# Second mixer's last output product by token halves, embedding matmuls back in the scan, the next stage begins with products of the left tokens

## The chip, the core and the metric

The kernel runs on one core of a Trainium2 chip. The metric is the device time of one execution in microseconds (us); of several runs the median counts.

## What is computed

One inference step of a two-layer decoder trunk for 512 prompt tokens and 64 sample tokens (8 sequences of 8) that share the weights; model width 1024, all in f32. Layer 0 has a mixer of two parallel heads (HGRN2 and RG-LRU), layer 1 a Mamba-2 mixer. Cut to what matters here:

```python
for i in range(DEPTH):                                   # 2 layers
    xn = _rmsnorm(x, W['g_mix'][i])
    mix = _even_mixer(xn, ...) if i % 2 == 0 else _odd_mixer(xn, ...)
    x = x + mix
    x = x + _swiglu(_rmsnorm(x, W['g_ffn'][i]), w1, w3, w2)
    x = x + _ple(x, p[i], W['ple_up'][i], W['ple_gate'][i], W['g_ple'][i])
y = _rmsnorm(x, W['g_final'])

# the end of _odd_mixer: a norm by each of 4 groups, then the out product
yg = y.reshape(B, L, G_C, D_INNER_C // G_C)
yg = yg * lax.rsqrt(jnp.mean(yg * yg, axis=-1, keepdims=True) + EPS)
out = (yg.reshape(B, L, D_INNER_C) * W['ssm_gnorm'][j]) @ W['ssm_out'][j]

def _swiglu(x, w1, w3, w2): return (jax.nn.silu(x @ w1) * (x @ w3)) @ w2
def _ple(x, p_i, w_up, w_gate, g):
    return _rmsnorm(jax.nn.sigmoid(x @ w_gate) * (p_i @ w_up), g)
```

## The kernel before

Activations lie features by tokens: `x[0]` to `x[7]` are 128 features by 576 tokens, and each product goes by two halves of 288 tokens (`half(s)`; the left half is s = 0). A product in f32 is made of three matmuls of fast type: every operand is split into a high and a low part, and high by high, low by high and high by low are added in PSUM. `wsplit` (L170) splits a weight tile of 128 x 1024, high part `whi` on ScalarE (L173), low part `wlo` on VectorE or GpSimd (L174); `split_to` does so with activations.

The order of the instructions is set by a scheduler of the language, engine by engine; code order, tile pools and their buffer counts are its input. An engine takes its own instructions strictly in that order.

`odd_mixer` (L705) runs 16 units of the scan (four groups of four). In a unit ScalarE makes `E`, the exponentials of the decay, VectorE multiplies it (L956), TensorE makes `yp` from it (L967), VectorE and GpSimd make `xs` from that, and ScalarE and VectorE split it into `xah` and `xal`, the operands `ya` of the out product. After a group's last unit its squares are summed (`acc`, `ssq` on TensorE), `ry` is a power on GpSimd (L236), and `rbc` on TensorE (L242) broadcasts it to all partitions; ScalarE copies it to SBUF (`rb`). `group_out` makes the out product of a group: for each of eight 128-feature blocks m 24 matmuls (both halves), the evacuation `t<-mm,rb` on VectorE (L348) and the add to `x` on GpSimd (L349). The table `OUT_AT` says behind which unit the group's product is written; the last group's stands behind unit 15, the last.

`ple_up` (L1227) makes the embedding product `p_i @ w_up`, 96 matmuls in each layer with evacuations `ev<-mm` on ScalarE (L1244). Its result is wanted only after the FFN. In layer 1 it is written behind the whole mixer and its operands are called `xb`.

`ffn` (L1042) makes the SwiGLU with a Strassen-like scheme: seven products replace eight, made of sums and differences of quarters of the activations (`b11`, `b21` from the left tokens, `b2`, `b1`, `b3`, `b4`, `b22` from differences or right tokens) and of the weights. The scaled quarters (x times the norm's weights, L1074, on VectorE) are `hh`; their splits are `bh` and `bl`. The norm factor `r` of the token is multiplied in afterwards, so that a product can run ahead of it. One product is 24 matmuls; the products' PSUM tiles are `mmx`, `mmy` and `mmz`, and `u` is a sum of weight quarters. Before, the first FFN products that TensorE takes stand behind the broadcast `rbc` of the norm factor.

Of the kernel before, what the change touches and what calls it, by code (L numbers as in the profile page):

```python
# [12 lines left out]
F = mybir.dt.float32  # L13
# [30 lines left out]
AHEAD, LAST, STEPS, UP_CUT = 4, 6, (3, 2), 6  # L44
PLE_V = [(0, 1, 2, 3, 4, 6), (0,)]
OUT_AT = {4: [(0, range(8))], 8: [(1, range(8))],
          12: [(2, range(0, 4))], 13: [(2, range(4, 6))], 14: [(2, range(6, 8))], 15: [(3, range(8))]}
XRB = 1
GT = [[4 * g, 4 * g + 1, 4 * g + 2, 4 * g + 3, 16 + g, 20 + g] for g in range(NG)]
LEVELS = (64, 32, 16, 8, 4, 2, 1)  # L50
# [29 lines left out]
def trunk(ctx, tc, a, stop=None):  # L80
# [21 lines left out]
    def pcol(name, i=0, n=1):  # L102
        return par[:, PAR[name] + i:PAR[name] + i + n]
# [29 lines left out]
    def bank(name="s", tag="s"):  # L133
        return pq.tile([P, 512], F, tag=tag, name=name)

    def singles(pool, tag):
        while True:
            yield [pool.tile([P, HF], R, tag=tag + t_, name=tag + t_, bufs=KD) for t_ in "hl"]
# [82 lines left out]
    def chunk(c):  # L221
        return slice(c * P, (c + 1) * P) if c < NCH else slice(SEQ, T)

    def rnorm(accs, n, lo, hi, outs):
        w = hi - lo
        nch = -(-w // P)
        last = w - (nch - 1) * P
        ps = bank("ssq")
        for i, acc in enumerate(accs):
            for c in range(nch):  # L230
                o = min(c * P, w - P)
                sums = PE.matmul(ps[:, c:c + 1], acc[:, o:o + P], ones[:, :1], start=(i == 0 and c == 0),  # L232
                                 stop=(i == len(accs) - 1 and c == nch - 1))
        ms, y = (tp.tile([P, nch], F, tag=n_, name=n_) for n_ in ("ms", "ry"))
        V.tensor_scalar(ms, ps[:, :nch], 1.0 / n, EPS, op0=OP.mult, op1=OP.add)
        G.tensor_tensor(y, ms, c_("mhalf", 1).to_broadcast([P, nch]), op=OP.pow)  # L236
        for b0 in range(0, w, 512):
            b1 = min(w, b0 + 512)
            pb = bank("rbc")
            for c0 in range(b0, b1, P):  # L240
                c1 = min(w, c0 + P)
                bc = PE.matmul(pb[:, c0 - b0:c1 - b0], y[:, c0 // P:c0 // P + 1].to_broadcast([P, P]), ident[:, P - (c1 - c0):],  # L242
                          start=True, stop=True)
            for out, sc in outs:
                S.activation(out[:, lo + b0:lo + b1], pb[:, :b1 - b0], AF.Copy, scale=sc)
        return sums.ins, bc.ins, pb

    def half(s):
        return slice(s * HF, (s + 1) * HF)
# [84 lines left out]
    def square_add(acc, src, first, eng=V):  # L334
        if first:
            S.activation(acc, src, AF.Square)
        else:
            sq = tmp("t2", 2)[:, :src.shape[-1]]
            one = S.activation(sq, src, AF.Square)
            two = eng.tensor_tensor(acc, acc, sq, op=OP.add)  # L340
            return one.ins, two.ins
# [33 lines left out]
    def even_mixer():  # L375
        xin = XIn("g_mix", 0)
        w_in, w_out = a["w_ein"], a["w_eout"]
        with ExitStack() as es:
# [323 lines left out]
                        next(fill[todo.pop(0)], None)  # L702
            run(mix_out(w_out, 0, split_out(oa, pairs(ac, "xc"))))

    def odd_mixer(xin, first):  # L705
        acts, r = xin.acts, xin.r
        w_in, w_out = a["w_sin"], a["w_sout"]
        with ExitStack() as es:
# [288 lines left out]
            def group_out(q, ms):  # L997
                run(mix_out(w_out, 4 * q.g, q.ya, q.rg, ms, q.marks if q.g == NG - 1 else ()))

            groups, xs, zs = {}, {}, {}  # L1000
            last_ya = singles(ac, "xa")
            units = 4 * NG

            def feed(u):
# [12 lines left out]
            for u in range(1 + GLOOK):  # L1017
                gate(u)
            scans = {}

            def step(u, n):
                if u >= units:
# [9 lines left out]
            for u in range(units):  # L1032
                for du, n in PIPE:
                    step(u + du, n)
                if u % 4 == 3:
                    group_norm(groups[u // 4])
                feed(u + LOOK)
                gate(u + 1 + GLOOK)
                for g_, ms in OUT_AT.get(u, []):
                    group_out(groups[g_], ms)  # L1040

    def ffn(i, ha):  # L1042
        w13, w2 = a["w13"][i], a["w2"][i]
        with tc.tile_pool(name=f"ffn{i}", bufs=1) as hp:
# [24 lines left out]
            (xg0, t0), (xg1, t1) = ([t_.bitcast(F) for t_ in hq()] for _ in range(2))  # L1069
            d3, d2, d1, d4 = t0[:, :, :HF], t0[:, :, HF:], t1[:, :, :HF], t1[:, :, HF:]  # L1070

            def scaled(xg, k0):
                for k in range(k0, k0 + 4):
                    V.tensor_scalar(xg[:, k - k0], x[k], pcol("g_ffn", i * KD + k), None, op0=OP.mult)  # L1074
                    square_add(acc, x[k], k == 0)

            scaled(xg0, 0)
            b11 = operand(0, xg0[:, :, :HF])
            V.tensor_tensor(d1, xg0[:, :, :HF], xg0[:, :, HF:], op=OP.subtract)
            b1 = operand(1, d1)  # L1080

            def lower():
                scaled(xg1, 4)
                bs = [operand(2, xg1[:, :, :HF])]
                V.tensor_tensor(d3, xg1[:, :, HF:], xg0[:, :, HF:], op=OP.subtract)
                V.tensor_tensor(d2, d3, xg0[:, :, :HF], op=OP.add)
                bs.append(operand(3, d2, -1.0))
                rnorm([acc], D, 0, T, [(r, 1.0)])
                bs.append(operand(4, d3))
                V.tensor_tensor(d4, d2, xg1[:, :, :HF], op=OP.subtract)  # L1090
                return bs + [operand(5, d4), operand(6, xg1[:, :, HF:])]

# [84 lines left out]
            for p0, p1 in PARTS:  # L1177
                hs = []
                dn = down(p0, p1, hs)
                for p in range(p0, p1):  # L1180
                    if p == p0:
                        ps, s1 = head(p)
                    if (p - p0) % 2 == 0:
                        hh, hl = hq()
                    o = 2 * ((p - p0) % 2)
                    xo = [ps[:, n, :HF] for n in range(2)]
                    if p == 0:
                        nxt = head(1)
                        wa = sums(0)
                        zs = q5(wa[1])  # L1190
                        b21, b2, b3, b4, b22 = lower()
                    ys = pre.pop("ys", None) or q2(p)
                    f1, f2 = hp.tile([P, T], F, tag="f1", name="f1", bufs=2), tmp("t2", 2)
                    block(s1, ys, f1[:, :HF], 0, 1.0)
                    if p:
                        wa = sums(p)
                    a21, a22, a11 = wa
                    u = wsum("u")
                    V.tensor_tensor(u, a22, a11, op=OP.add)
                    prod(xo, wsplit(u, KD, wp, 2), b2, False)  # L1200
                    s2 = copied(ps, "t2")
                    if p:
                        zs = q5(a22)
                    else:
                        pre["ys"] = q2(1)
                    nc.gpsimd.dma_start(a21, w13[p, 0], accum_op=OP.add)
                    prod(xo, wsplit(a21, KD, wp, 2), b3, False)
                    s3 = copied(ps, "t1")
                    block(s3, zs, f2[:, HF:], 1, -1.0)
                    if p and p + 1 < p1:  # L1210
                        nxt = head(p + 1)
                    elif p:
                        next(dn)
                    prod(xo, wload(w13[p, 3], KD), b4, False)
                    V.tensor_tensor(f2[:, :HF], xo[0], r[:, :HF], op=OP.mult)
                    S.activation(f2[:, :HF], f2[:, :HF], AF.Silu, scale=-1.0)
                    V.scalar_tensor_tensor(f2[:, :HF], xo[1], -1.0, f2[:, :HF], op0=OP.mult, op1=OP.mult)
                    split_to((hh[:, o + 1], hl[:, o + 1]), f2)
                    nc.gpsimd.dma_start(u, w13[p, 1], accum_op=OP.add)  # L1219
                    prod(zs, wsplit(u, KD, wp, 2), b22, False)  # L1220
                    block(s2, zs, f1[:, HF:], 1, 1.0)
                    split_to((hh[:, o], hl[:, o]), f1)
                    hs += [(hh[:, o + 1], hl[:, o + 1]), (hh[:, o], hl[:, o])]
                    ps, s1 = nxt
                run(dn)
# [141 lines left out]
    for i in range(2):  # L1367
        if i == 0:
            even_mixer()
        else:  # L1370
            odd_mixer(mid, first)
        if stop == 3 * i:
            return dump()
        with tc.tile_pool(name=f"plea{i}", bufs=WPRE) as ha:
            if i == 0:
                ev, *_ = ple_up(i, singles(ac, "xa"), ha)
                places = None
            else:
                places = (quads(ha, "xb", 2), singles(ac, "xa"))
                ev, *_ = ple_up(i, quads(ha, "xb", 2))  # L1380
            ffn(i, ha)
            if stop == 3 * i + 1:
                return dump()
            if i == 0:
                first = ple(i, ha, ev, mid.half, None, (mid, [a["w_dt"], a["w_sin"][32], a["w_sin"][36]]))
            else:
                ple(i, ha, ev, final, places)
        if stop == 3 * i + 2:
            return dump()
# [112 lines left out]
```

## Time and profile before

| | us |
|---|---|
| median of 3 runs | 1849.98 |
| the runs | 1845.04, 1849.98, 1851.35 |
| the profiled execution | 1847.01 |
| its span | 1845.2 |
| TensorE busy in it | 1737.6 (94%) |
| VectorE busy | 1322.2 (72%) |
| ScalarE busy | 813.1 (44%) |
| GpSimd busy | 481.1 (26%) |

TensorE is the engine with the most work, so a place where it idles, or where its granted clock is below full, is a place where the time can change. Busy time of the other engines counts only where TensorE waits for them.

### The profile page before, as it was taken

How to read it: one execution, taken by the hardware profiler on the slowest of the kernel's cores; microseconds unless marked ns; L12 is line 12 of the kernel's file. 1: busy time of each engine (PE TensorE's matmuls, PEld its weight loads, DVE VectorE, ACT ScalarE, POOL GpSimd, SP SyncE). 2: the span in 40 equal slices, each digit the busy share in tenths (PEclk: the TensorE clock that was granted, in tenths of full speed). 3: DMA queues.
4: the chain of work that ended last, by engine and by line, in shares of the span. 5: the costliest groups of instructions: out<-in, count | busy, mean ns of one | idle time of the engine just before them, and what ended most of it. 6: DMA issues, size and time to landing. Idle time of an engine off the chain costs nothing.

```text
span 1845.2 us, 32297 instructions
## 1 busy us (share of the span) xinstructions
PE 1737.6 (94%) x13134; PEld 1687.8 (91%) x13134; DVE 1322.2 (72%) x2189; ACT 813.1 (44%) x1343; POOL 481.1 (26%) x456
## 2 busy tenths in 40 slices
PE   7899989899999999989998999999789999999995
PEld 7789889899999999989987999998679999999994
DVE  6876774776577476578995896988677657647656
ACT  6654542554154144344553444544355425414432
POOL 3442444200000000032445547356530000000003
PEclk9999999999999999999998999999789999999997
DMA  5111212365465463312331322323326446546321
GB/s 194 46 71 65 70 47 102 109 177 139 125 190 137 131 169 83 119 54 73 110 114 66 107 101 89 118 83 109 99 75 177 132 127 186 146 124 172 83 81 52
DMA packets 66293, 205.29 MB, mean 111 GB/s; under 512 B 7393, under 2 KB 13153, under 8 KB 66145
## 3 DMA queue, kind: packets, MB, share of 16 engines
q1 hardware_dynamic: 59232, 179.57, 28.2%
q0 software_dynamic: 6336, 23.07, 7.4%
q8 instruction: 103, 1.69, 0.4%
q10 hardware_dynamic: 576, 0.59, 0.1%
q14 instruction: 46, 0.37, 0.1%
HBM read 188.64 MB, written 14.56 MB: 110 GB/s over the span
## 4 chain that ended last, share of the span: by engine, by line
PE 76%; DVE 15%; ACT 5%; issue 2%; POOL 2%; DMA 0%; SPq 0%; POOLq 0%; DVEq 0%; ACTq 0%
PE mm L192 22%; PE mmx L1106 15%; PE mm L1150 15%; PE mmz L1106 8%; PE mmy L1106 4%; PE mmg L192 3%; POOL ry L236 1%; PE rbc L242 1%; DVE cu L808 1%; PE lev L560 1%; PE ssq L232 1%; ACT whi L173 1%; DVE x L1263 1%; PE yp L967 1%; DVE wlo L174 1%
## 5 line engine op out<-in xcount | busy, mean ns | idle before, releaser
L173 ACT ACTIVATE whi<-wraw 128x1024 fp32r<-128x1024 f32 (+2 forms) x207 | 215.2, 1040 | 361.9 <-PE mm L1150 164.4
L174 DVE TENSOR_TENSOR wlo<-wraw,whi 128x1024 fp32r<-128x1024 f32 (+1 forms) x181 | 224.6, 1241 | 75.2 <-ACT whi L173 73.8
L1106 PE MATMUL mmx<-bh,whi 128*128 128x288 f32 x704 | 208.4, 296 | 3.9 <-ACT t L1111 3.9
L1106 PE MATMUL mmx<-bl,whi 128*128 128x288 f32 x704 | 207.7, 295 | 0.0
L1106 PE MATMUL mmx<-bh,wlo 128*128 128x288 f32 x704 | 207.2, 294 | 0.0
L192 PE MATMUL mm<-xah,whi 128*128 128x288 f32 x632 | 193.9, 307 | 5.1 <-DVE t L348 3.0
L192 PE MATMUL mm<-xal,whi 128*128 128x288 f32 x632 | 190.6, 302 | 0.0
L192 PE MATMUL mm<-xah,wlo 128*128 128x288 f32 x632 | 190.4, 301 | 0.0
L192 PE MATMUL mm<-xch,whi 128*128 128x288 f32 x536 | 161.4, 301 | 2.1 <-DVE x L351 2.0
L192 PE MATMUL mm<-xch,wlo 128*128 128x288 f32 x536 | 160.9, 300 | 0.0
L192 PE MATMUL mm<-xcl,whi 128*128 128x288 f32 x536 | 160.6, 300 | 0.0
L348 DVE TENSOR_TENSOR t<-mm,rb 128x288 f32<-128x288 f32 x160 | 66.6, 452 | 123.7 <-PE mm L1150 104.8
L1106 PEld LDWEIGHTS mmx<-bh,whi 128*128 128x128 f32 x704 | 132.0, 187 | 4.9 <-ACT t L1111 4.9
L1150 PE MATMUL mm<-hh,whi 128*128 128x288 f32 x616 | 133.4, 296 | 2.3 <-DVE t L348 2.3
L1106 PEld LDWEIGHTS mmx<-bh,wlo 128*128 128x128 f32 x704 | 132.5, 188 | 0.0
L1150 PE MATMUL mm<-hh,wlo 128*128 128x288 f32 x616 | 132.3, 295 | 0.0
L1106 PEld LDWEIGHTS mmx<-bl,whi 128*128 128x128 f32 x704 | 132.1, 188 | 0.0
L1150 PE MATMUL mm<-hl,whi 128*128 128x288 f32 x616 | 131.8, 295 | 0.0
L192 PEld LDWEIGHTS mm<-xah,whi 128*128 128x128 f32 x632 | 121.2, 192 | 11.0 <-ACT bh L158 2.6
L192 PEld LDWEIGHTS mm<-xal,whi 128*128 128x128 f32 x632 | 121.1, 192 | 1.5 <-issue 1.1
L192 PEld LDWEIGHTS mm<-xah,wlo 128*128 128x128 f32 x632 | 121.1, 192 | 1.0 <-issue 0.5
L1219 POOL DMA_DIRECT2D u<-w x22 | 19.1, 868 | 349.9 <-DVE wlo L174 349.9
(500 smaller groups left out, 5034.2 us busy)
## 6 DMA issues: line engine op xcount, KB each, us to landing
wraw<-w SPq DMA_DIRECT2D x98, 512.0 KB, 3.5
a<-w SPq DMA_DIRECT2D x66, 512.0 KB, 3.8
wraw<-w_sin SPq DMA_DIRECT2D x40, 512.0 KB, 3.3
wraw<-w_ein SPq DMA_DIRECT2D x22, 512.0 KB, 3.2
a<-w POOLq DMA_DIRECT2D x22, 512.0 KB, 5.2
u<-w POOLq DMA_DIRECT2D x22, 512.0 KB, 5.1
wraw<-wg SPq DMA_DIRECT2D x16, 512.0 KB, 3.2
s<-ss SPq DMA_DIRECT2D x16, 512.0 KB, 3.6
```

What stands on the lines that cost most here:

```text
L173: S.activation(hi, raw, AF.Copy)
L174: eng.tensor_tensor(lo, raw, hi.bitcast(F), op=OP.subtract)
L192: PE.matmul(ps, w[:, cols], v, start=(k == 0 and i == 0), stop=(k == n - 1 and i == 2))
L232: sums = PE.matmul(ps[:, c:c + 1], acc[:, o:o + P], ones[:, :1], start=(i == 0 and c == 0), stop=(i == len(accs) - 1 and c == nch - 1))
L236: G.tensor_tensor(y, ms, c_("mhalf", 1).to_broadcast([P, nch]), op=OP.pow)
L242: bc = PE.matmul(pb[:, c0 - b0:c1 - b0], y[:, c0 // P:c0 // P + 1].to_broadcast([P, P]), ident[:, P - (c1 - c0):], start=True, stop=True)
L348: V.tensor_tensor(t, src, r[:, half(s)], op=OP.mult)
L560: PE.matmul(ps[:, chunk(c)], lhs[:, chunk(c)], rhs[:, chunk(c)], start=True, stop=True)
L808: V.scalar_tensor_tensor(uc, up[:, k:k + TC], cw[:, 24 * k + i:24 * k + i + 1], uc, op0=OP.mult, op1=OP.add)
L1106: PE.matmul(outs[n], w[:, o], v, start=(first and k == 0 and t_ == 0), stop=(k == 3 and t_ == 2), skip_group_check=not first)
L1150: PE.matmul(ps[:, s_, :HF], w[:, k * P:(k + 1) * P], v[:, half(s_)], start=(k == 0 and t_ == 0), stop=(k == n - 1 and t_ == 2))
L1219: nc.gpsimd.dma_start(u, w13[p, 1], accum_op=OP.add)
```

## The change

Three things are changed. Both layers' FFN begins otherwise: the scaled copies run on ScalarE by halves, `b11` and `b21`, which need the left tokens alone, come first, and the products with them stand ahead of everything that needs the right tokens or `r`; the squares are added by halves. In layer 1 the embedding's 96 matmuls are written into the last two units of the scan (entry -1 in the table; operands `pa`). And the last group's out product goes by token halves: all eight blocks m for the left tokens, then all for the right; the left adds to `x` run on GpSimd, the right ones on VectorE; the weights of blocks 4 to 7 are kept in the mixer's `ya` buffers (`wo`).

```diff
-          12: [(2, range(0, 4))], 13: [(2, range(4, 6))], 14: [(2, range(6, 8))], 15: [(3, range(8))]}
+          12: [(2, range(0, 4))], 13: [(2, range(4, 6))], 14: [(-1, range(2)), (2, range(6, 8))], 15: [(-1, range(6)), (3, range(8))]}
...
+            upper = ple_up(1, iter_pa(hp))
+            ev = next(upper)
...
+            def last_out(q):
+                wts, marks, i = [], q.marks[:2], 0
+                for m2 in range(KD // 2):
+                    raw = wp.tile([P, 1024], F, tag="raw", name="wraw", bufs=RAW)
+                    nc.sync.dma_start(raw.rearrange("p (m c) -> p m c", m=2),
+                                      w_out[2 * m2:2 * m2 + 2, :, 4 * q.g * P:(4 * q.g + 4) * P].rearrange("m p c -> p m c"))
+                    if m2 < 2:
+                        hi, lo = wsplit(raw, KD, wp, 2)
+                        wts += [(hi[:, o:o + SEQ], lo[:, o:o + SEQ]) for o in (0, SEQ)]
+                    else:
+                        for o in (0, SEQ):
+                            dst = [hp.tile([P, T], R, tag="ya", name="wo", bufs=YB)[:, :SEQ] for _ in range(2)]
+                            wts.append(split_to(dst, raw[:, o:o + SEQ]))
+                for s in range(2):
+                    for m in range(KD):
+                        if m % 2 == 0:
+                            ps = pm.tile([P, 2, 512], F, tag="mm", name="mm")
+                        with after_all(*marks[i:i + 1]):
+                            mm_half(ps[:, m % 2, :HF], [wts[m]], q.ya, s)
+                        i += 1
+                        t = tmp("t1", 2)[:, :HF]
+                        V.tensor_tensor(t, ps[:, m % 2, :HF], q.rg[:, half(s)], op=OP.mult)
+                        (V if s else G).tensor_tensor(x[m][:, half(s)], x[m][:, half(s)], t, op=OP.add)
...
-            def scaled(xg, k0):
+            def scaled(xg, k0, hf):
                 for k in range(k0, k0 + 4):
-                    V.tensor_scalar(xg[:, k - k0], x[k], pcol("g_ffn", i * KD + k), None, op0=OP.mult)
-                    square_add(acc, x[k], k == 0)
-
-            scaled(xg0, 0)
+                    S.activation(xg[:, k - k0, half(hf)], x[k][:, half(hf)], AF.Copy, scale=pcol("g_ffn", i * KD + k))
+                    square_add(acc[:, half(hf)], x[k][:, half(hf)], k == 0)
+
+            scaled(xg0, 0, 0)
             b11 = operand(0, xg0[:, :, :HF])
-            V.tensor_tensor(d1, xg0[:, :, :HF], xg0[:, :, HF:], op=OP.subtract)
-            b1 = operand(1, d1)
-
-            def lower():
-                scaled(xg1, 4)
-                bs = [operand(2, xg1[:, :, :HF])]
+            scaled(xg1, 4, 0)
+            b21 = operand(1, xg1[:, :, :HF])
+
+            def right():
+                scaled(xg0, 0, 1)
+                V.tensor_tensor(d1, xg0[:, :, :HF], xg0[:, :, HF:], op=OP.subtract)
+                scaled(xg1, 4, 1)
                 V.tensor_tensor(d3, xg1[:, :, HF:], xg0[:, :, HF:], op=OP.subtract)
                 V.tensor_tensor(d2, d3, xg0[:, :, :HF], op=OP.add)
-                bs.append(operand(3, d2, -1.0))
-                rnorm([acc], D, 0, T, [(r, 1.0)])
-                bs.append(operand(4, d3))
+                bs = [operand(2, d2, -1.0)]
+                rnorm([acc], D, 0, T, [(r, 1.0)], "o")
+                bs += [operand(3, d1), operand(4, d3)]
...
+                    ys = pre.pop("ys", None) or q2(p)
                     if p == 0:
                         nxt = head(1)
-                        wa = sums(0)
-                        zs = q5(wa[1])
-                        b21, b2, b3, b4, b22 = lower()
-                    ys = pre.pop("ys", None) or q2(p)
+                        b2, b1, b3, b4, b22 = right()
                     f1, f2 = hp.tile([P, T], F, tag="f1", name="f1", bufs=2), tmp("t2", 2)
                     block(s1, ys, f1[:, :HF], 0, 1.0)
-                    if p:
-                        wa = sums(p)
-                    a21, a22, a11 = wa
+                    if p == 0:
+                        pre["ys"] = q2(1)
+                    a21, a22, a11 = sums(p)
...
-                ev, *_ = ple_up(i, quads(ha, "xb", 2))
```

ScalarE at the start of the second layer's FFN, before. Rows give the line, the operation, and out<-in; `t<-x` are squares of x, `bh` the high parts of the operands, `ev` evacuations of the embedding.

```order
L339 ACTIVATE t_14578<-x_76 128x576
...
L158 ACTIVATE bh<-hh 128x1152
L158 ACTIVATE bh<-hl 128x1152
...
L339 ACTIVATE t_14716<-x_82 128x576
L1244 ACTIVATE ev<-mm 128x288 x2
L158 ACTIVATE bh<-hh 128x1152
```

The same place on ScalarE now, from the last squares on; `hh<-x_75` to `hh<-x_82` are the scaled copies, first all left halves, then all right ones.

```order
L339 ACTIVATE t_14777<-x_81 128x288
L1116 ACTIVATE hh<-x_75,par 128x288
...
L1116 ACTIVATE hh<-x_82,par 128x288
L1116 ACTIVATE hh<-x_75,par 128x288
...
L1116 ACTIVATE hh<-x_82,par 128x288
L339 ACTIVATE t_14781<-x_82 128x288
L158 ACTIVATE bh<-hh 128x1152 x2
```

The scaled copies are new on ScalarE (before, they stood on VectorE), and the first split `bh` stands behind all sixteen; the first of them waits for the last matmul of the out product.

TensorE in the last unit of the scan, before:

```order
L939 MATMUL cbs<-chl,sel 64x64 x2
L951 MATMUL cb<-chl,sel 128x512 x2
L963 MATMUL yq<-es,xd 64x64 x2
L967 MATMUL yp<-E,xd 64x128 x4
L969 MATMUL yp<-Ec,st 64x128 x2
```

And now, where `pa` is the embedding's operand:

```order
L960 MATMUL cb<-chl,sel 128x512 x2
L192 MATMUL mm<-pa,whi 128x288 x2
L192 MATMUL mm<-pa,wlo 128x288
L192 MATMUL mm<-pa,whi 128x288
L972 MATMUL yq<-es,xd 64x64 x2
...
L192 MATMUL mm<-pa,wlo 128x288
L976 MATMUL yp<-E,xd 64x128 x4
```

Embedding matmuls now stand between the scan's products of the last unit, where before one followed the other; more stand behind `yp` and ahead of the sums of squares.

TensorE around the broadcast of the first layer's FFN, before (`xah`, `xal` are the embedding's operands there):

```order
L192 MATMUL mm<-xal,whi 128x288
L192 MATMUL mm<-xah,wlo 128x288
L242 MATMUL rbc<-cst,ry 128x128 x4
L242 MATMUL rbc<-cst,ry 128x64
L192 MATMUL mm<-xah,whi 128x288
```

And now:

```order
L1149 MATMUL mmy<-bh,whi 128x288
L1149 MATMUL mmy<-bl,whi 128x288
L242 MATMUL rbc<-cst,ry 128x128 x4
L242 MATMUL rbc<-cst,ry 128x64
L1149 MATMUL mmy<-bh,wlo 128x288
```

The broadcast moved from the middle of the embedding's matmuls into the fourth of the FFN's products.

## Rows read from the trace of the kernel before

**Rows 1.** The page: TensorE in 40 equal slices, tenths busy; the evacuations' group.

```profile
PE   7899989899999999989998999999789999999995
...
L348 DVE TENSOR_TENSOR t<-mm,rb 128x288 f32<-128x288 f32 x160 | 66.6, 452 | 123.7 <-PE mm L1150 104.8
```

**Rows 2.** Busy us by stretches: PE, PEld, DVE, ACT, POOL, clock, DMA share, GB/s.

```profile
340.00:350.00 10.00, 9.65 (x74) 9.28 (x72) 10.00 (x14) 8.26 (x17) 2.37 (x1) 1.00 0.18 62
350.00:360.00 10.00, 4.90 (x25) 4.80 (x25) 4.09 (x8) 3.14 (x10) 5.14 (x1) 0.66 0.12 44
...
1290.00:1300.00 10.00, 6.11 (x51) 4.53 (x50) 8.11 (x18) 6.91 (x19) 8.14 (x6) 0.89 0.17 65
1300.00:1310.00 10.00, 3.26 (x28) 2.85 (x28) 2.80 (x2) 2.30 (x6) 3.20 (x2) 0.50 0.16 50
1310.00:1320.00 10.00, 8.04 (x41) 8.07 (x42) 5.79 (x10) 2.47 (x7) 2.11 (x2) 0.58 0.48 166
...
1340.00:1350.00 10.00, 8.95 (x58) 8.48 (x57) 10.00 (x14) 2.78 (x4) 5.83 (x5) 0.89 0.16 52
...
1360.00:1370.00 10.00, 4.08 (x19) 4.08 (x20) 4.81 (x10) 4.00 (x12) 5.87 (x1) 0.66 0.13 52
```

**Rows 3.** TensorE's timeline, second mixer's end: start, us, operation, idle before and releaser.

```profile
1296.78 0.30 PE L939 MATMUL cbs<-chl,sel 128*64 128x64 f32 x2 [2.44 <-DVE s L932]
...
1303.93 1.12 PE L967 MATMUL yp<-E,xd 128*64 128x128 f32 x8 [4.52 <-DVE E L956]
...
1311.96 2.27 PE L232 MATMUL ssq<-cst,acc 128*128 128x1 f32 x10 [4.78 <-DVE acc L989]
...
1339.11 0.58 PE L192 MATMUL mm<-xah,whi 128*128 128x288 f32 x1 [2.41 <-DVE t L348]
```

**Rows 4.** TensorE's timeline at both FFN starts.

```profile
345.65 1.17 PE L232 MATMUL ssq<-cst,acc 128*128 128x1 f32 x10
...
355.20 2.40 PE L242 MATMUL rbc<-cst,ry 128*128 128x128 f32 x10 [5.10 <-POOL ry L236]
...
374.17 0.30 PE L1106 MATMUL mmx<-bh,whi 128*128 128x288 f32 x1
...
1355.28 1.17 PE L232 MATMUL ssq<-cst,acc 128*128 128x1 f32 x10
...
1365.92 2.39 PE L242 MATMUL rbc<-cst,ry 128*128 128x128 f32 x10 [6.17 <-POOL ry L236]
...
1381.57 0.30 PE L1106 MATMUL mmy<-bh,whi 128*128 128x288 f32 x1
...
1384.74 0.30 PE L1106 MATMUL mmx<-bh,whi 128*128 128x288 f32 x1
```

**Rows 5.** GpSimd's timeline: powers ry and adds to x.

```profile
1314.51 1.18 POOL L236 TENSOR_TENSOR ry<-ms,cst 128x5 f32<-128x5 f32 x1 [5.05 <-DVE ms L235]
...
1321.52 0.80 POOL L349 TENSOR_TENSOR x<-x,t 128x288 f32<-128x288 f32 x1 [2.81 <-DVE t L348]
...
1343.01 2.69 POOL L349 TENSOR_TENSOR x<-x,t 128x288 f32<-128x288 f32 x2 [1.66 <-DVE t L348]
...
1358.28 7.59 POOL L236 TENSOR_TENSOR ry<-ms,cst 128x5 f32<-128x5 f32 x1 [6.14 <-DVE ms L235]
```

**Rows 6.** VectorE's timeline: the product with E; first and last of five groups.

```profile
1301.82 2.05 DVE L956 TENSOR_TENSOR E<-E,gm 128x1024 f32<-128x1024 f32 x1 [2.08 <-ACT E L955]
...
1358.12 1.21 DVE L174 TENSOR_TENSOR wlo<-wraw,whi 128x1024 fp32r<-128x1024 f32 x1
...
1363.26 1.55 DVE L159 TENSOR_TENSOR bl<-hh,bh 128x288 fp32r<-128x288 f32 x4
```

**Rows 7.** ScalarE's timeline: a pair of scaled copies, a split of an operand.

```profile
1309.49 0.96 ACT L161 ACTIVATE xah<-xs,kp 128x288 fp32r<-128x288 f32 x2 [7.70 <-POOL xs L974]
...
1358.15 1.17 ACT L161 ACTIVATE bh<-hl 128x1152 fp32r<-128x1152 f32 x1 [1.15 <-DVE hl L1086]
```

**Rows 8.** DMA issues by line: count, KB each, median us to landing.

```profile
wraw<-w_sout SPq DMA_DIRECT2D x16, 512.0 KB, 3.8
```

More of the change, by code (lines that the diff above doesn't have):

```diff
@@ L222, in chunk, with rnorm @@
         return slice(c * P, (c + 1) * P) if c < NCH else slice(SEQ, T)
-    def rnorm(accs, n, lo, hi, outs):
+    def rnorm(accs, n, lo, hi, outs, tag="s"):
         w = hi - lo
@@ L227, in rnorm @@
         last = w - (nch - 1) * P
-        ps = bank("ssq")
+        ps = bank("ssq", tag)
         for i, acc in enumerate(accs):
@@ L238, in rnorm @@
             b1 = min(w, b0 + 512)
-            pb = bank("rbc")
+            pb = bank("rbc", tag)
             for c0 in range(b0, b1, P):
@@ L703, in even_mixer, with iter_pa @@
             run(mix_out(w_out, 0, split_out(oa, pairs(ac, "xc"))))
+    def iter_pa(hp):
+        for tag, bufs, w in (("up", UPB, TP), ("cu", 1, TP)):
+            two = []
+            for j in range(2):
+                t = hp.tile([P, w], R, tag=tag if tag == "up" or not j else "bf", name="pa", bufs=bufs)[:, :T]
+                two.append([t[:, half(s)] for s in range(2)])
+            for s in range(2):
+                yield [two[0][s], two[1][s]]
     def odd_mixer(xin, first):
@@ L1019, in odd_mixer @@
             scans = {}
+            def last_out(q):
[11 more added lines that the diff above has]
+                            wts.append(split_to(dst, raw[:, o:o + SEQ]))
+                for s in range(2):
+                    for m in range(KD):
[7 more added lines that the diff above has]
+                        (V if s else G).tensor_tensor(x[m][:, half(s)], x[m][:, half(s)], t, op=OP.add)
             def step(u, n):
@@ L1039, in odd_mixer @@
                 for g_, ms in OUT_AT.get(u, []):
-                    group_out(groups[g_], ms)
+                    if g_ < 0:
+                        for m in ms:
+                            next(upper)
+                    elif g_ == NG - 1:
+                        last_out(groups[g_])
+                    else:
+                        group_out(groups[g_], ms)
+        return ev
     def ffn(i, ha):
@@ L1201, in ffn @@
                     s2 = copied(ps, "t2")
[L1202 to L1205, printed above, removed]
+                    zs = q5(a22)
                     nc.gpsimd.dma_start(a21, w13[p, 0], accum_op=OP.add)
@@ L1370, in trunk @@
         else:
-            odd_mixer(mid, first)
+            ev = odd_mixer(mid, first)
         if stop == 3 * i:
```

## The prediction

> **What bounds the kernel now.** I read the page first, then the busy time by stretches, then TensorE's timeline where it idles, then the engines that it waits for. The page's slices show TensorE at nine tenths nearly everywhere, so only the dents can give time back; the deepest, at slices 28 and 29 of the 40, is the second mixer's end and the start of its feed-forward stage (FFN) [rows 1]. By stretches [rows 2] TensorE is busy 3.26 us of 10 in 1300-1310 at clock 0.50, 8.04 in 1310-1320 at 0.58, 4.08 in 1360-1370 at 0.66; the first layer's FFN start has one dent, 4.90 of 10 at 0.66. The timeline names the waits [rows 3]: 2.44 us before the last unit's products, 4.52 for E from VectorE, 4.78 for acc, then 2.41 inside the out product. At both FFN starts TensorE waits 5.10 and 6.17 us for the row norm's power ry on GpSimd before it may broadcast r [rows 4].
>
> All matmuls stay, so the sum needs only two markers: the first matmul of product u in each FFN, with the same work ahead of it in both kernels, at 374.17 and 1384.74 [rows 4]. A product of 24 matmuls takes 1384.74 - 1381.57 = 3.17 us at full clock, 0.132 each. What stands behind the markers keeps its order and its price.
>
> **First FFN.** The sum-of-squares matmuls start at 345.65 [rows 4]; with 48 embedding matmuls behind them at 0.132 and 0.7 for themselves the embedding ends at 352.7, in both kernels. Before, the broadcast then stands in the middle of this work and costs 5.10 idle, and the stretch's clock of 0.66 another 4.90 x 0.34 = 1.7. Now products of the left tokens (mmx and mmy of the first two heads) stand ahead of the broadcast, and ry has some 12 us in which VectorE waits between its sums. I count: 0.35 for the last evacuation, four products 12.7, sums of squares 0.4, broadcast 1.2, and 1.1 for the second head's weight split, which needs a buffer that frees at the first product's last matmul and takes 1.06 on ScalarE and then some on VectorE: 352.7 + 15.8, marker near 368.7, **5.4 us gained**. The scaled copies leave VectorE, which is busy throughout 340-350, for ScalarE, which there is busy 8.26 of 10 [rows 2]; sixteen half copies at 0.44 (below) are 7.0 us more, most of them earlier, as each half of x comes, so I charge nothing. That cover is thin: the bounds are 6.8 gained, if the split is hidden too, and 2, if half of the 7.0 delays embedding evacuations.
>
> **Second mixer's scan.** The 96 embedding matmuls, 96 x 0.132 = 12.7 us, move from behind the out product into the waits of 2.44, 4.52 and 4.78 (11.7 us). They bring with them four copies of the embedding input and two weight splits on ScalarE and VectorE, sixteen evacuations on ScalarE, and DMA issues on SP. The chain of the scan, E on ScalarE, its product on VectorE (2.05 [rows 6]), yp, xah, acc, is queued behind some of them: one split and two evacuations stand ahead of E, about 1.0 us in all, and the first copy of the late out weights stands ahead of xah, behind a DMA of 3.8 us from issue [rows 8] whose issue waits for a split. Against that yp, which before ran at clock 0.50 (28 matmuls busy 3.26 us in 1300-1310 [rows 2]), runs at full clock and saves 1.6. I set the sums of squares at 1311.6 (before: 1311.96 [rows 3]). Nothing of the chain gets faster, so the floor is about 1310; the other end is one more DMA landing late, 1315.5.
>
> **Out product by halves.** 192 matmuls from 1312.2 at 0.132 are 25.4 us, with 1.0 for sums and broadcast. Its waits are not in the trace, so I bound them. (a) The second half of the late weights lands before the first evacuation on VectorE, 1.2 us. (b) Sixteen steps of 12 matmuls share two PSUM tiles, and in the new order 7 of the last 14 steps wait for the evacuation of the step just ahead; an evacuation is 0.45 [rows 1] plus a release, I take 0.75: 5.3 us. Ends: 0, if the order's waits fall on tiles already read, and 14 x 0.75 = 10.5. (c) About 2.5 us of it at half clock, more than in 1340-1350, which behind the wait of 2.41 had clock 0.89 over 8.95 us [rows 2], 1.0 lost. The last out matmul ends at 1312.2 + 25.4 + 1.0 + 1.2 + 5.3 + 2.5 = **1347.6**.
>
> One thing more lies on this path. The left halves' adds to x go to GpSimd, one by one with new square adds on VectorE. Two such adds took 2.69 us at 1343.01, one 0.80 at 1321.52 [rows 5], and a late add holds the temporary that the next evacuation writes. The Trainium skill's page "SBUF — State Buffer", section "SBUF: two separate sides", says that VectorE's operations with two SBUF inputs and GpSimd's that read SBUF hold a shared port pair by an exclusive lock. That speaks against this split of work; by it the eight adds would cost up to 8 x 0.55 = 4.4 us more and the result would be 1840, whereas I have left them at the price of the lone one.
>
> **Second FFN, where the change costs.** Before, the scaled copies ran on VectorE as each x came ready, half a product behind. In the new order the first copy on ScalarE waits for the last out matmul of all: the late out weights lie in the mixer's ya buffers, whose memory the FFN reuses. And all 16 half copies, left and right, stand ahead of the first operand split. From the last out matmul T: 0.3 of release, 16 x 0.44 = 7.0 (a pair of scaled 288-wide copies takes 0.96, so one more costs 0.44 [rows 7]), 0.4 of square, 1.1 of split bh [rows 7]: the first mmx at T + 8.8, and the other 23 wait for the low part, two differences and a split behind it on VectorE, until T + 10.5. 23 matmuls with 1.5 lost to a clock that the idle stretch let fall (the broadcast after 6.17 of idle took 2.39): T + 15.0; mmy T + 17.9. Now r is wanted. ry starts near T + 14.4, and VectorE again runs four operations on SBUF operands without a gap, as in 1358.12 to 1364.8, where ry took 7.59 instead of 1.18 [rows 5, 6]; I let it end about 1.0 after the run, at T + 20.9. Broadcast 1.2, two products 6.4: marker at T + 28.5 = 1376.1. **8.6 us gained**. Had ry its 1.18, nothing would wait: 3.0 more. Were a half copy 0.52: 1.3 less. The loads a2, a3 and a0 also wait for T, but are wanted only behind the marker.
>
> **Sum.** 5.4 + 8.6 = 14.0 us, off the profiled 1847.0: 1833.0. The median of the runs (1849.98) lies 3.0 above the profiled one, so I forecast **1836**. With the bounds: losses of 3.4 in the first FFN, 5.2 in (b), 3.9 in the scan, 1.3 in the copies, hardly all at once; gains of 1.4, 5.3 and 3.0. I take 1828 to 1846 for the likeliest case.
>
> **Rivals.**
> 1. Better, 1828: the steps' waits are on tiles already read and ry slips in. For it: before, the same 192 matmuls with the same two tiles met one wait above a microsecond [rows 3]; against it: there an evacuation was released two steps ahead, and now the order names the step just ahead. 1836 - 5.3 - 3.0.
> 2. Paid back, 1847: what goes into the scan's waits lengthens them. ScalarE and VectorE take each queue in order, and a split that waits for a late weight holds E, xah or acc. The sums of squares come at 1315.5 (3.9 later) and all 14 steps wait (5.2 more), GpSimd's adds add 2: 1836 + 11. For it: VectorE is 8.11 and ScalarE 6.91 busy in 1290-1300 [rows 2]; against it: in 1300-1310 they are busy 2.80 and 2.30 [rows 2]. It is also the case in which the change does not do what it says, since in the second layer the left-first start is not there: the order holds it behind the right half.
> 3. Slower, 1862: the clock. Steps of 1.6 us with stops of 0.75 leave TensorE 68% busy; should it run the whole out product at half speed, that is 192 x 0.11 = 21 us, with 5.2 for the remaining stops. It decides once some 130 of the matmuls run slowly: 14.0 of gain, less 5.2, and 5.5 below the line is 14.3 / 0.11. For it: clock 0.50 at 3.26 of 10 busy; against it: 0.89 at 8.95 [rows 2].
>
> **How the numbers follow.** Forecast 0.60, better 0.14, paid back 0.16, slower 0.10. Three tenths of a per cent, 5.5 us, is what a measurement can tell here, so the lines are 1844.5 and 1855.5. The forecast and the better case fall below the first (0.74), the paid-back case between (0.16), the clock case above (0.10). The range 1826 to 1848 leaves out the clock case and the edges of the others.
>
> **What would show it.** Right: no idle over 2 us on TensorE in 1296-1312, full clock there; marker of the first FFN near 368.7 with the broadcast unwaited; TensorE idle about 8.8 us behind the last out matmul, with sixteen copies on ScalarE in it; ry long in the second FFN, short in the first; marker near 1371 to 1379. Wrong: a clock near 0.5 through the out product, sums of squares later than 1314, stops at every step, or an FFN copy that starts before the out product ends.

## The result

| | before | after |
|---|---|---|
| median of 6 runs, us | 1850.09 | 1839.22 |
| the runs, us | 1845.04 to 1851.36 | 1835.75 to 1843.60 |
| ratio after to before | | 0.9943 (95%: 0.9928 to 0.9958) |
| span of the profiled execution | 1845.2 | 1837.7 |

The change makes the kernel 10.9 us faster (by the interval 7.8 to 13.3), where 14 were forecast; the sign and the range held. The traces show that the forecast was nearer than its working deserved: the two stages that were to give 14.0 us gave 5.8 between the traced executions, because of two steps that the sum had mispriced, and a slip in its bookkeeping hides this when the predicted times are held against the trace.

Busy time of the changed kernel by stretches answers to [rows 2]; the columns are the same.

```profile
330.00:340.00 10.00, 9.79 (x53) 9.82 (x54) 6.12 (x12) 6.20 (x13) 0.00 (x0) 0.69 0.32 122
350.00:360.00 10.00, 9.37 (x69) 8.95 (x68) 9.44 (x18) 8.28 (x21) 0.00 (x0) 1.00 0.32 104
...
1280.00:1290.00 10.00, 10.00 (x82) 8.80 (x82) 6.49 (x15) 4.16 (x12) 4.66 (x3) 0.74 0.20 61
1300.00:1310.00 10.00, 8.71 (x78) 7.94 (x76) 4.85 (x7) 6.46 (x15) 3.28 (x2) 1.00 0.31 105
1320.00:1330.00 10.00, 8.12 (x58) 7.45 (x56) 4.53 (x10) 2.11 (x5) 3.48 (x5) 1.00 0.01 2
1350.00:1360.00 10.00, 3.17 (x12) 2.78 (x13) 7.31 (x7) 9.49 (x17) 0.93 (x1) 0.50 0.67 201
```

The dents moved rather than closed. 350-360 and 1300-1310 are filled (4.90 and 3.26 before), but 330-340 and 1280-1290 now run at clock 0.69 and 0.74, and 1350-1360 is a new hole at 0.50. TensorE's timeline shows what opens each; it answers to [rows 3, 4].

```profile
330.21 0.58 PE L192 MATMUL mm<-xch,whi 128*128 128x288 f32 x1 [3.20 <-DVE x L351]
...
365.10 1.22 PE L242 MATMUL rbc<-cst,ry 128*128 128x128 f32 x10
...
368.86 0.30 PE L1149 MATMUL mmx<-bh,whi 128*128 128x288 f32 x1
...
1278.85 0.85 PE L192 MATMUL mm<-pa,whi 128*128 128x288 f32 x2 [2.49 <-ACT pa L158]
...
1303.10 0.66 PE L976 MATMUL yp<-E,xd 128*64 128x128 f32 x8 [0.71 <-DVE E L965]
...
1310.88 1.25 PE L232 MATMUL ssq<-cst,acc 128*128 128x1 f32 x10 [1.09 <-DVE acc L998]
...
1325.58 0.37 PE L192 MATMUL mm<-xah,wo 128*128 128x288 f32 x1 [0.71 <-DVE t L1053]
...
1356.38 0.61 PE L1149 MATMUL mmx<-bh,whi 128*128 128x288 f32 x1 [8.39 <-ACT bh L158]
...
1376.74 0.30 PE L1149 MATMUL mmx<-bh,whi 128*128 128x288 f32 x1
```

In the first FFN the broadcast waits for nothing any more, but 3.20 us are lost earlier, at 330. In the scan the waits of 4.52 and 4.78 are down to 0.71 and 1.09, and 2.49 us are spent on the embedding operand pa. The out product stops eight times for an evacuation (0.71 is one of the stops, 5.3 us in all), and the second FFN starts 8.39 us behind it.

To compare kernels stage by stage without what happened ahead, two stretches are read off TensorE's timeline in every trace below. **A** runs from the sums of squares at the even mixer's end (300.18 before) to those at the end of layer 0 (780.73): 480.55 us before, 477.94 after; layer 0's FFN lies in it. **B** runs from the last-but-one yi product of the scan (1264.33 before) to layer 1's first gate matmul (1762.48): 498.15 before, 494.93 after; the end of the scan, the last out product and the second FFN lie in it.

### The profile page after: what moved, and what is told of

Its sections match the earlier page's. It is cut to its first block, busy times and chain, and to the rows that moved or that the text cites. A ratio compares the mean times of both kernels' runs of the same rounds, so it can differ in the third digit from the quotient of the medians.

```text
span 1837.7 us, 32351 instructions
## 1 busy us (share of the span) xinstructions
PE 1740.4 (95%) x13134; PEld 1689.4 (92%) x13134; DVE 1316.2 (72%) x2201; ACT 828.4 (45%) x1393; POOL 453.7 (25%) x444
## 4 chain that ended last, share of the span: by engine, by line
PE 78%; DVE 12%; ACT 6%; issue 2%; DMA 1%; POOL 1%; SPq 0%; POOLq 0%; DVEq 0%; ACTq 0%
PE mm L192 24%; PE mmx L1149 15%; PE mm L1193 15%; PE mmz L1149 8%; PE mmy L1149 4%; PE mmg L192 3%; ACT whi L173 1%; DVE cu L817 1%; PE ssq L232 1%; PE lev L560 1%; PE rbc L242 1%; DVE x L1301 1%; PE yp L976 1%; PE ds L919 1%; DVE wlo L174 1%
## 5 line engine op out<-in xcount | busy, mean ns | idle before, releaser
L1149 PE MATMUL mmx<-bh,whi 128*128 128x288 f32 x704 | 209.7, 298 | 12.7 <-ACT bh L158 8.4
L192 PE MATMUL mm<-xah,whi 128*128 128x288 f32 x600 | 183.5, 306 | 4.6 <-DVE t L1053 2.2
L192 PE MATMUL mm<-xal,whi 128*128 128x288 f32 x600 | 181.0, 302 | 0.0
L192 PE MATMUL mm<-xah,wlo 128*128 128x288 f32 x600 | 180.4, 301 | 0.0
L348 DVE TENSOR_TENSOR t<-mm,rb 128x288 f32<-128x288 f32 x144 | 59.6, 451 | 125.1 <-PE mm L1193 104.9
L1149 PEld LDWEIGHTS mmx<-bh,whi 128*128 128x128 f32 x704 | 133.0, 189 | 14.1 <-ACT bh L158 8.6
L192 PEld LDWEIGHTS mm<-xah,whi 128*128 128x128 f32 x600 | 114.5, 191 | 10.2 <-DVE t L1053 2.9
L192 PEld LDWEIGHTS mm<-xal,whi 128*128 128x128 f32 x600 | 114.7, 191 | 2.0 <-issue 1.4
L192 PEld LDWEIGHTS mm<-xah,wlo 128*128 128x128 f32 x600 | 114.7, 191 | 1.1 <-issue 0.7
L192 PEld LDWEIGHTS mm<-xch,whi 128*128 128x128 f32 x536 | 102.5, 191 | 5.3 <-issue 3.8
```

The lines of the kernel that those rows point to most:

```text
L192: PE.matmul(ps, w[:, cols], v, start=(k == 0 and i == 0), stop=(k == n - 1 and i == 2))
L348: V.tensor_tensor(t, src, r[:, half(s)], op=OP.mult)
L1149: PE.matmul(outs[n], w[:, o], v, start=(first and k == 0 and t_ == 0), stop=(k == 3 and t_ == 2), skip_group_check=not first)
```

## Experiments

My theory from these traces: the three parts are worth more apart than together. The halves of the out product lose what they were to win, since their late weights hold the FFN's memory, and two waits of VectorE beside GpSimd cost the rest. The rival: the parts need each other. All ratios are to the kernel before, with their 95% intervals.

| run | ratio | A | B |
|---|---|---|---|
| the change | 0.9943 (0.9928 to 0.9958) | 477.9 | 494.9 |
| e1 embedding only | 0.9945 (0.9927 to 0.9962) | 480.9 | 488.5 |
| e2 FFN only | 0.9939 (0.9922 to 0.9956) | 479.3 | 491.1 |
| e3 change without halves | 0.9908 (0.9890 to 0.9926) | 475.9 | 487.1 |
| e4 change without FFN | 0.9955 (0.9939 to 0.9970) | 481.4 | 491.2 |
| e5 halves, weights split twice | 0.9906 (0.9891 to 0.9921) | 478.8 | 485.7 |
| e6 embedding all in unit 15 | 0.9997 (0.9984 to 1.0009) | 477.9 | 501.9 |
| e7 change, layer 0's low parts | 0.9917 (0.9899 to 0.9934) | 473.2 | 493.9 |
| e8 as e3, and these low parts | 0.9886 (0.9868 to 0.9904) | 473.8 | 485.9 |
| e9 as e5, and these low parts | 0.9881 (0.9860 to 0.9901) | 472.4 | 486.1 |
| e10 as e8, group 2's low parts too | 0.9893 (0.9875 to 0.9910) | 473.0 | 486.3 |

Where layer 0's code is the same, A varies between traces: 480.6 to 481.4 with the old FFN (three), 475.9 to 479.3 with the new (five), 472.4 to 473.8 with the low parts moved (four). The sets do not overlap. The step of 4.9 us between the means of the last two is larger than the widest spread inside a set, 3.4; the step of 3.0 between the first two is not.

### e1, e2: one part alone

e1 has the embedding in the scan and the old out product and FFN:

```diff
+          12: [(2, range(0, 4))], 13: [(2, range(4, 6))], 14: [(-1, range(2)), (2, range(6, 8))], 15: [(-1, range(6)), (3, range(8))]}
...
-                ev, *_ = ple_up(i, quads(ha, "xb", 2))
```

> The kernel before with one part of the change: the embedding matmuls written into the last two units of the scan; last out product and FFN as before. Theory (the three parts are worth something each, the embedding part filling 11.7 us of waits but paying some 4 us for a longer scan): 1842 to 1844, sums of squares of the last group 3 to 5 us later than in the kernel before less nothing, TensorE idle near 2.5 us before the first embedding matmul. Rival (the fill costs nothing): 1838, sums of squares at about 1311.

Measured 1840.75, just better than the theory's window: B falls by 9.7 us, and the sums of squares come 1.3 us later behind the yi product than before, not 3 to 5. The fill works, and the longer scan takes little of it back.

e2 has the new FFN beginning alone:

```diff
+                    S.activation(xg[:, k - k0, half(hf)], x[k][:, half(hf)], AF.Copy, scale=pcol("g_ffn", i * KD + k))
```

> The kernel before with the new FFN beginning alone, in both layers; embedding and out product as before. Theory: 3 to 5 us gained in the first layer, and 5 to 6 in the second, where the copies need not wait for late out weights and the broadcast no longer stalls TensorE: 1840 to 1842. Rival (the left-first order needs the out product by halves in the second layer): 3 to 5 us in all, 1845 to 1847.

Measured 1839.51: B falls by 7.0, A by 1.3. The left-first order is worth more in the second layer than in the first, without the halves. Each of these two parts alone gives as much as the whole change.

### e3, e4: one part left out

e3 is the change without `last_out`:

```diff
-                    elif g_ == NG - 1:
-                        last_out(groups[g_])
```

> The changed kernel without the out product by halves: the last group goes block by block with both halves, as before; no late weights in the ya buffers. Theory (the halves cost more than they give: stops of 0.6 at 7 steps and 8.4 us of idle before the FFN): faster than the changed kernel by 4 to 8 us, 1831 to 1835. Rival (halves pay): 1841 to 1845, slower than the changed kernel.

Measured 1833.87, as the theory said: without the halves B is 7.9 us shorter than in the changed kernel, 5.1 of it behind the sums of squares. TensorE's timeline of e3 at the second FFN:

```profile
1341.23 0.37 PE L1123 MATMUL mmx<-bh,whi 128*128 128x288 f32 x1 [1.19 <-issue]
...
1365.43 0.40 PE L1123 MATMUL mmx<-bh,whi 128*128 128x288 f32 x1 [3.11 <-ACT t L1128]
...
1373.83 2.40 PE L242 MATMUL rbc<-cst,ry 128*128 128x128 f32 x10 [2.66 <-POOL ry L236]
```

The first product starts 1.19 us behind the out product instead of 8.39; some of it is lost again at 1365 and at the broadcast. In e2, where the embedding still stands between the out product and the FFN, no wait there is above 1.13 us. The gains of e1 and e2 (9.7 and 7.0) come to 11.1 together and not to 16.7.

e4 is the change with the FFN of before, of whose edit two lines stand here:

```diff
-                    S.activation(xg[:, k - k0, half(hf)], x[k][:, half(hf)], AF.Copy, scale=pcol("g_ffn", i * KD + k))
+                    V.tensor_tensor(d1, xg0[:, :, :HF], xg0[:, :, HF:], op=OP.subtract)
```

> The changed kernel with the FFN of before in both layers: embedding in the scan and out product by halves stay. Theory: the old scaled copies wait for the last out matmul too, and the broadcast stalls TensorE in both layers: 1846 to 1852. Rival (the FFN part gives little): 1840 to 1843.

Measured 1842.26, inside the rival's window: the FFN part adds little to the other two. B is 2.7 us longer than in e1, which lacks only the halves: they cost with the old FFN too, but less.

### e5: the halves without the late weights

```diff
-                        for o in (0, SEQ):
-                            dst = [hp.tile([P, T], R, tag="ya", name="wo", bufs=YB)[:, :SEQ] for _ in range(2)]
+                for s in range(2):
+                    for m in range(KD):
+                        if m % 2 == 0:
...
+                            hi, lo = wsplit(raw, KD, wp, 2)
```

> The changed kernel with the out product still by token halves, but its weights loaded and split once for each half in the ordinary rotating buffers, none kept in the mixer's ya buffers (four more loads and eight splits more than needed). Theory (the idle of 8.4 us before the FFN comes from the memory that the late weights hold): the first scaled copy starts in the middle of the out product, idle before the first mmx below 2 us, 1832 to 1835. Rival (the halves themselves cost, by their stops and the order on ScalarE): 1837 to 1841.

Measured 1834.52. The scaled copies on ScalarE in the changed kernel, all in one row, and in e5, the first and the eighth:

```profile
1348.03 6.92 ACT L1116 ACTIVATE hh<-x,par 128x288 f32<-128x288 f32 x16 [0.67 <-PE mm L192]
```

```profile
1322.92 0.54 ACT L1110 ACTIVATE hh<-x,par 128x288 f32<-128x288 f32 x1 [2.95 <-POOL x L1048]
...
1339.27 0.52 ACT L1110 ACTIVATE hh<-x,par 128x288 f32<-128x288 f32 x1
```

In the changed kernel all sixteen wait for TensorE's last out matmul and take 6.92 us while it idles. In e5 they wait for GpSimd's add of x and run inside the out product; TensorE's first FFN product then waits 1.46 us, for a weight, and stands ahead of the last out matmuls. B is 9.2 us shorter than in the changed kernel, 8.1 of it behind the sums of squares, although e5 loads and splits all four of the group's weight tiles a second time. So the halves themselves don't cost; the memory of their late weights does. The edit also changes when weights are split, so the 9.2 are not all the memory's.

### e6: where the embedding stands

```diff
-          12: [(2, range(0, 4))], 13: [(2, range(4, 6))], 14: [(-1, range(2)), (2, range(6, 8))], 15: [(-1, range(6)), (3, range(8))]}
+          12: [(2, range(0, 4))], 13: [(2, range(4, 6))], 14: [(2, range(6, 8))], 15: [(-1, range(8)), (3, range(8))]}
```

> The changed kernel with all eight steps of the embedding written into the last unit of the scan, none into the one before. Theory (the embedding's first matmuls, queued ahead of the last unit's scan products, cost about 4 us: 2.5 us of idle for the split operand and a stretch at clock 0.74): no idle above 1.5 us for pa, sums of squares 2 to 4 us earlier, 1835 to 1838. Rival (the waits it would have filled come back): within 1.5 us of the changed kernel.

Both expectations fell: the kernel is as slow as before. TensorE's timeline of e6:

```profile
1302.31 0.33 PE L972 MATMUL yq<-es,xd 64*64 64x64 f32 x4
1309.52 0.66 PE L976 MATMUL yp<-E,xd 128*64 128x128 f32 x8
...
1317.92 2.26 PE L232 MATMUL ssq<-cst,acc 128*128 128x1 f32 x10 [6.65 <-DVE acc L998]
```

All the embedding now stands ahead of yp. Forty-eight of its matmuls run from 1302.57 to yp, which is on the chain, and nothing is left for the wait behind it: 6.65 us of idle. The wait of 2.5 us at unit 14 is then for `es`, not for pa, as in the kernel before. Of the 7.0 us by which B is longer than in the change, 3.2 lie ahead of the sums of squares; the rest lies behind them, where the code is that of the change, and is not explained by the embedding's place. The two steps in unit 14 of the change are what leaves embedding matmuls for the place behind yp.

### e7, e8: the first layer's stall

The low parts of the later out weights of layer 0 (in both of its out products) move from GpSimd to VectorE, in the changed kernel (e7) and in e3 (e8):

```diff
-                hi, lo = wsplit(raw, KD, wp, 2, eng=G if POOL_LO else V)
+                hi, lo = wsplit(raw, KD, wp, 2, eng=G if POOL_LO and (r is not None or m < 4) else V)
```

> The changed kernel with the low parts of the later weights of layer 0's out product (blocks 4 to 7 of each of its two parts) made on VectorE, not on GpSimd. Theory (the 3.2 us idle before 330 comes from VectorE's sum u, which took 4.26 us beside a GpSimd split instead of 1.2): that sum takes 1.2 to 1.5, the idle is below 1, first FFN marker 2 to 4 us earlier, 1835 to 1837. Rival (VectorE has too much to do there anyway): marker within 1 us, time unchanged.

VectorE's sum `u` and GpSimd's split in the changed kernel, then the same sum in e7:

```profile
323.44 4.26 DVE L1240 TENSOR_TENSOR u<-a,a 128x1024 f32<-128x1024 f32 x1
```

```profile
323.89 2.71 POOL L174 TENSOR_TENSOR wlo<-wraw,whi 128x1024 fp32r<-128x1024 f32 x1
```

```profile
326.34 1.22 DVE L1240 TENSOR_TENSOR u<-a,a 128x1024 f32<-128x1024 f32 x1
```

The sum ended 1.1 us after GpSimd's split (326.60) in the one, although its record begins 0.45 us ahead of the split's, and took its own 1.22 in the other. With it the idle at 330 fell from 3.20 to 1.28 (below 1 was expected), and the ratio from 0.9943 to 0.9917; these two intervals still overlap, the sets of A do not. The theory holds, with an effect in A (4.9 by the sets) somewhat larger than expected. Not all of it is this sum's: TensorE's broadcast inside the even mixer, ahead of it, already comes 0.5 us earlier, and the kernel before ran the sum beside a split too, in 2.69 us.

> The changed kernel without the out product by halves, and with the low parts in layer 0 on VectorE as in the run before this one. Theory (the two gains are in different layers and add): 1829 to 1832. Rival (layer 0's is eaten by VectorE): 1833 to 1835, as without it.

Measured 1831.96: 0.9886, as if the gains add.

### e9, e10: the two together, and the lock at pa

e9 has the edits of e5 and of e7 together, no others.

> The out product by halves with its weights split once for each half (nothing kept in ya), and layer 0's later low parts on VectorE. Theory (the two gains lie in different layers and add): 1829 to 1831, like the kernel without halves and with the same low parts. Rival: 1833 to 1835.

Measured 1827.79, just below the theory's window, ratio 0.9881: with and without the halves the kernel is equally fast once nothing holds the memory, and both are faster than the change (the intervals don't meet).

e10 moves group 2's last low parts to VectorE as well:

```diff
-                hi, lo = wsplit(raw, KD, wp, 2, eng=G if POOL_LO and (r is not None or m < 4) else V)
+                hi, lo = wsplit(raw, KD, wp, 2, eng=G if POOL_LO and (r is not None or m < 4) and len(ms) != 2 else V)
```

> The kernel without halves and with layer 0's low parts on VectorE, and in addition the low parts of the last four blocks of group 2's out product (units 13 and 14) on VectorE, so that no GpSimd split runs beside VectorE's splits of the embedding operand pa, which took 4.04 us for four in the changed kernel. Theory (part of the 4 us by which the scan got longer is that lock): pa's four take 1.6 to 2.2 us, sums of squares of the last group 1 to 3 us earlier, 1828 to 1831. Rival (the embedding operand's late arrival and the order on TensorE set it, or VectorE lacks the time): no change within 1 us, or slower.

In the changed kernel pa's splits and, in e10, the first of them and the wait on TensorE:

```profile
1278.35 4.04 DVE L159 TENSOR_TENSOR pa<-ev,pa 128x288 fp32r<-128x288 f32 x4
```

```profile
1276.63 0.46 DVE L159 TENSOR_TENSOR pa<-ev,pa 128x288 fp32r<-128x288 f32 x1 [1.40 <-ACT pa L158]
```

```profile
1279.21 0.54 PE L192 MATMUL mm<-pa,whi 128*128 128x288 f32 x2 [3.53 <-ACT pa L158]
```

The splits are short now (1.7 us for four), and it gives nothing: B is 486.3 against e8's 485.9, and TensorE waits 3.53 us where it waited 2.23. Its wait ends on ScalarE's third high part of pa, and ScalarE had waited 1.86 us for the operand's DMA and then made E and a weight split ahead of that part. The rival was right; the lock was real and not on the path.

## Why the prediction came out as it did

**The bookkeeping** failed first. The two markers came at 368.86 and 1376.74, where 368.7 and 1376.1 were written, and that looks exact. But 1376.1 was worked out in the times of the kernel before, from its 1311.96, without the 5.4 us that the first layer was to give; with them it had to be 1370.7 in the new trace. Counted from the scan's yi product, the second layer gave 3.2 us where 8.6 were summed: 4.1 us are missing in the scan, 1.1 in the out product and 0.25 in the FFN. The terms of the first FFN add to 368.5, where 368.7 is written.

**First FFN**: forecast 5.4, measured 2.6 in this pair and 3.0 by the sets of A. The end went as said: a short stop for the second head's split, a broadcast that waits for nothing, a short ry. GpSimd's ry after and, below it, the one of the second FFN:

```profile
361.99 1.19 POOL L236 TENSOR_TENSOR ry<-ms,cst 128x5 f32<-128x5 f32 x1 [35.39 <-DVE ms L235]
```

```profile
1363.19 5.90 POOL L236 TENSOR_TENSOR ry<-ms,cst 128x5 f32<-128x5 f32 x1 [7.64 <-DVE ms L235]
```

What failed is the embedding's end at 352.7 "in both kernels", and with it the sentence "so I charge nothing", which weighed ScalarE's copies alone. Behind the even mixer's sums of squares the embedding ends after 56.3 us, where the sum has 52.5; from there to the marker it is 15.1, where 15.8 were summed. The moved work changed the order on VectorE, u's sum fell beside a GpSimd split, and the evacuations of the out product behind it let TensorE idle 3.20 us and then run at 0.69. The result lies inside the bounds, 2 to 6.8, but the cause named with the lower one was not it: from 330.21 to the FFN's first product TensorE waits for no evacuation longer than 0.16 us, so ScalarE's copies were not late. In e7, without the split beside u, the embedding ends after 51.6 us.

**Scan**: this is the mis-sized term. Sums of squares at 1310.88 seem earlier than the 1311.6 forecast, but the stage was entered 4.82 us earlier (yi at 1259.51 against 1264.33): in the old times 1315.7, 4.1 late, and just past the far end named, 1315.5. It is the scan's share of the rival "paid back", in full. Full clock at yp and idles near 1 us in 1296-1312 came as said. From yi to the sums of squares it is 47.6 us before and 51.4 in the change: TensorE is busy 14.1 us longer, where the embedding's matmuls were put at 12.7, and its idle falls by 10.4, from 16.0 to 5.6. Of the 11.7 us of waits that were to be filled 2.2 are left. The 2.49 for pa are no new idle, since the kernel before waits as long in unit 14, for `es`, which the sum did not name:

```profile
1282.19 0.33 PE L963 MATMUL yq<-es,xd 64*64 64x64 f32 x4 [2.46 <-DVE es L945]
```

The clock, which was to give 1.6 back at yp, took 1.1 more: busy time times the missing share of the clock adds to 2.1 us before and 3.2 in the change. This part is spread between traces. e7 has the same code there as the change, and as far behind its yi as the change's row of 1280-1290 with clock 0.74, it shows:

```profile
1279.04:1289.04 10.00, 10.00 (x93) 9.15 (x92) 7.84 (x18) 4.56 (x11) 4.66 (x3) 0.90 0.20 61
```

The other runs agree. From yi to the sums of squares it is 48.4 to 48.9 us in e1, e3, e8, e9 and e10, with 4.2 to 4.9 of idle and 1.7 lost to the clock. It is 49.8 in e4 and e7, which keep the late weights, with 5.2 to 5.4 of idle and as little lost to the clock; and 50.2 in e5, which has the code of e9 there, with 4.5 of idle but 3.2 lost. So of the change's 51.4 about 1 us goes with the late weights, whose copy on ScalarE stands behind its DMA and ahead of xah (about 1.2 us), and 1.5 is the clock of that execution. The old scan spreads too: e2 has it, with 48.8 and 3.3 lost.

**Out product**: T, the end of the last out matmul, came at 1348.0, 37.1 behind the sums of squares where 36.0 were summed. The first of the eight stops, 1.01 us, waits for the copied broadcast; the seven others make 4.25, where 7 x 0.75 = 5.3 were summed. The low clock fell ahead of the stops (0.83 in 1310-1320) and was back at 1.00 in 1320-1350: the clock rival, priced at 1862, didn't happen, with TensorE 81% busy in 1320-1330. What made the stage 1.1 us longer than summed all the same is not placed. GpSimd's adds took 0.80 each, so the shared port of the Trainium skill's page "SBUF — State Buffer", section "SBUF: two separate sides", did not delay them; it showed at u, at pa and at ry instead. Beside the adds VectorE ran its evacuations, which read one operand from PSUM; its operations on two SBUF operands began at most 0.5 us before an add ended, and took 0.57 or 0.80 us then where they take 0.46 alone.

**Second FFN**: first product at T + 8.4 (8.8 said), copies 6.92 (7.0), ry held till the end of VectorE's run, marker T + 28.75 (28.5). The mechanism was read from the order and is right, and the sum was right to 0.3 us, this with some luck: TensorE's first products ended at T + 19.5, where 17.9 was summed, and the wait for ry, 1.65 in place of 3.0, covered the difference. From the sums of squares to the end of B it is 443.6, 447.3 and 444.1 us in the kernels with the new FFN that keep the late weights (the change, e6, e7), and 435.5 to 438.4 in the five that do not (e3, e5, e8, e9, e10). So this step is also what cost the change most.

Between the traced pair A and B sum to 5.8 us and the spans differ by 7.5, while the runs differ by 10.9; executions of one kernel spread over 6 to 8 us, part of it ahead of A (the two traces are 2.7 apart at 300), so the single pair says less than the sets. Where the rest of the 10.9 was gained is not shown, and that the forecast came so near to it is in part luck.

## What to carry to other kernels

Before work is moved forward, ask whose memory its operands will hold: a buffer that is borrowed from a closing pool makes everything that opens there wait for its last reader, and a stage that is to start early then starts last. Filler for a wait has to stand on both sides of the chain's own instructions, since an engine takes its queue in order: e6, with all of it ahead of yp, gave back the whole gain. And a sum over two places is made in one count of time: shift the second by what the first is to give.

## What the hardware showed that I had not expected

VectorE's 128x1024 sum of two SBUF operands took 4.26 us beside a 2.71 us GpSimd split, and 1.22 alone; it ended 1.1 us after GpSimd was done, although its record begins first. The other way round ry on GpSimd took 5.90 in a run of VectorE operations on SBUF operands and 1.19 in a gap. The eight adds on GpSimd kept their 0.80 us beside VectorE's evacuations from PSUM.

A wait of TensorE of about 2.5 us in unit 14 was followed by a granted clock of half in e2 and not in the kernel before, which has the same code there. Between executions of the same code in this stretch the loss to the clock differs by 1.2 us (before and e2) and 1.5 (the change and e7, e5 and e9), which is as much as several of the effects looked for.
